# Decoder layer: GpSimd makes part of the low halves of the weights, and two more matrix products use the wide seven-product scheme

## The chip, the cores and the metric

One core of a Trainium2 chip runs the whole program. The metric is the device time of one execution, in microseconds. In the text PE is TensorE (matmul), DVE is VectorE, ACT is ScalarE, POOL is GpSimd, and SP is SyncE, which only issues transfers.

## The reference, cut to what matters

256 tokens of width 2048 go through one layer. The token mixers' part is left out here, since the change touches it in one place only.

```python
def rmsnorm(x, g):
    xf = x.astype(jnp.float32)
    y = xf * lax.rsqrt(jnp.mean(xf * xf, axis=-1, keepdims=True) + EPS)
    return (y * g.astype(jnp.float32)).astype(x.dtype)
...
h = rmsnorm(x, attn_norm[l])
proj = h @ w_in[l]
...
y_gla = (o_gla * jax.nn.silu(gr)) @ w_br_gla[l]
y_sb = stick_breaking_mixer(...) @ w_br_sb[l]
y_mem = memory_mixer(q_m, m_k, m_v) @ w_br_mem[l]
g = jax.nn.sigmoid(gates.reshape(B, T, N_BRANCH, D))
merged = g[:, :, 0] * y_gla + g[:, :, 1] * y_sb + g[:, :, 2] * y_mem
x = x + merged @ w_o[l]
h2 = rmsnorm(x, ffn_norm[l])
gate, up = jnp.split(h2 @ w_gate_up[l], 2, axis=-1)
x = x + (jax.nn.silu(gate) * up) @ w_down[l]
```

The feed-forward width is 5632. All inputs are float32, and so are the results.

## The kernel before

**High and low parts.** A matmul of float32 takes its operands rounded to fp32r. To keep the precision, every operand is split into a high part and a low part (`split`, L148): ACT casts `hi` (L151), and DVE subtracts it from the source to give `lo` (L152). A product is then three matmuls, high by high, high by low and low by high (`mm`, L268, L270, L271 in `sgemm`; L224 to L226 in `gemm`). The weights arrive as raw tiles of four chunks (a chunk is 128 of the inner dimension; the tile is 128x2048, 1024 KB). They are split two chunks at a time, 128x1024, into a pair of tiles `wh` and `wl`. From the output projection on there are six such pairs, handed out in turn (`parts`), and a pair comes free when PE has used it.

**The wide product.** `sgemm` (L233) computes two blocks of 512 columns for both halves of the tokens. The first two raw tiles of each block, 8 chunks of inner dimension, go through a scheme of seven products instead of eight (a form of Strassen's): sums of token operands are made ahead (`make_forms`, the "forms" `sh`/`sl` or `sd`), and sums of weight tiles on the way. `p` says how many chunks of a tile take part: with `p` of 4 all of them, with 2 half, and the other half goes through plain `rest` steps (the lists `l21`, `l11`, `l22`, `l12`). A unit of a product is two chunks: one split, and 2 x 3 matmuls. A `rest` step is also one split of two chunks, and 2 x 2 x 3 matmuls, for both token halves. So for each chunk in the scheme seven products of three matmuls stand where eight would.

The seven products are named by one letter in the table `seq`, which sets the order of work: `a` (p1, tile 21), `b` (p2, tile 11), `e` (p3, tile 12), `f` (q4, tile 11 after tile 21 was added to it), `g` (p5, tile 21 minus or plus 22), `h` (p6, plus 12), `i` (p7, tile 22 after 12 was added to it). `r0` and `r1` are the `rest` steps of the two blocks. The sums that change the tile in place for a product are DVE's (L283); those for `f` and `i` are transfers that accumulate, issued on POOL's queue (L331, L351), if `moved` is set and the product is not `late`. `late` is for a product whose token operand has just been made: the forms are waited for at `(made,)`, behind some of the rests, and `f`'s sum is DVE's.

**What sets the order elsewhere.** Small tasks (transposes of new operands, making of forms) are generators in a list `background`; `step` advances the first of them once behind each unit. The framework then orders each engine's queue; each engine runs its queue in order and waits on the others by semaphores.

**The places that matter.** The memory branch's result comes back from DRAM through `fetch_out` (L668), beside the small matmuls for `gaT` (L990, L994). The output projection `w_o` is two `sgemm` calls (L1110); it makes `x2` (L1116), which is transposed (L457) and split into `hh` and `hl` (L154, L155), and the forms of these are made (L420, L152). Eleven gate-and-up groups (L1142) and six calls for the down projection (L1169) follow, in three parts: groups 0 to 3, 4 to 7, 8 to 10, each part with two down calls. The first gate group has `p` of 2 and is `late`; the last down call (`end`) has `p` of 2. The down forms `sd` are made beside the third group of a part. Results of down calls but the last two are added to `x2d` in DRAM by POOL's accumulating transfers (L1177); the last two add to `x2s` in SBUF and go out (L1183, L1185).

Of the kernel before, what the change touches and what calls it, by code (L numbers as in the profile page):

```python
# [77 lines left out]
def trunk(ctx: ExitStack, tc: tile.TileContext, a, out):  # L78
# [68 lines left out]

    def split(hi, lo, src, scale=None):  # L148

        if scale is None:  # L150
            act.copy(hi, src)  # L151
            dve.tensor_tensor(lo, src, hi.bitcast(F32), op=ALU.subtract)  # L152
        else:
            act.activation(hi, src, AF.Copy, scale=scale)  # L154
            dve.scalar_tensor_tensor(lo, src, scale, hi.bitcast(F32), op0=ALU.mult, op1=ALU.subtract)  # L155
# [76 lines left out]

    def sgemm(xs, forms, w, blks, p, row0=0, late=False, moved=True, base=None, end=False):  # L233

# [37 lines left out]

        def half(raw, g):
            wh, wl = (x[:].rearrange("p (k n) -> p k n", k=2) for x in parts())
            split(wh, wl, raw[:, g : g + 2])
            return wh, wl

        def prod(dst, left, b, last, *sums):

            for g in range(0, p, 2):  # L280
                for to, of in sums:
                    x, y = (q[i][0][:, g : g + 2] for i in (to, of))
                    dve.tensor_tensor(x, x, y, op=ALU.add)  # L283
                wh, wl = half(q[b][0], g)
                for i in range(2):
                    mm(dst, left[g + i], wh[:, i], wl[:, i], last and g + i == p - 1)
                step()
# [72 lines left out]
        def rest(j, k, last):  # L360
# [4 lines left out]
            raw, g, done = loaded[j, k]  # L365
            wh, wl = half(raw, g)
            if done:
# [13 lines left out]
        if late == "forms":  # L381
            seq = [a, *l21, *r1[:1], b, *l11, *r0, *r1[1:2], (made,), g, *l22, h, e, *l12, *r1[2:3], i, f, *r1[3:]]
        elif late:
            seq = [a, *l21, b, *l11, *r0, *r1[:1], (made,), g, *l22, *r1[1:2], h, e, *l12, *r1[2:3], i, f, *r1[3:]]
        elif end:
            seq = [a, *l21, *r0, g, h, *l22, b, *l11, e, *l12, i, f, *r1]
        else:
            seq = [a, *l21, *r0[:2], g, *r0[2:], h, *l22, b, *l11, e, *l12, *r1[:2], i, *r1[2:3], f, *r1[3:]]
# [282 lines left out]
    def fetch_out(o, place):  # L671
        high, low = place

        def work():
# [3 lines left out]
            yield  # L678
            for c in range(0, 8, 4):
                split(high[:, c : c + 4], low[:, c : c + 4], v[:, c : c + 4])  # L680
                if c == 4:
                    done()
                yield
# [304 lines left out]
    for k, x in enumerate(xs):  # L988
        for i in range(2):
            pe.matmul(p[: 2 * GR, :T], w_ga[:, k], x[i], start=k + i == 0, stop=(k, i) == (KD - 1, 1))  # L990
        if k % 8 == 7:
            step()
    gaT = gl.tile([2 * GR, T], F32, name="gaT", bufs=1)
    dve.tensor_copy(gaT[:], p[: 2 * GR, :T])  # L994
    flush()
    background.append(steps)
# [108 lines left out]
    for n0 in range(0, D, 2 * NB):  # L1105
        xr = []
        for n in (n0, n0 + NB):
            xr.append(gog.tile([P, 2, NB], F32, name="xr", tag="g_og"))
            nc.sync.dma_start(xr[-1][:], a["x"][:, n : n + NB].rearrange("(t p) n -> p t n", p=P))
        for j, result in sgemm(ms, sm_, a["w_o"], (n0 // NB, n0 // NB + 1), SP, late=n0 == 0):  # L1110
            if x2 is None:
# [27 lines left out]
    for part in (range(0, 4), range(4, 8), range(8, NF)):  # L1139
        fs, tiles = [], []  # L1140
        for i in part:
            for j, result in sgemm(hs, sf, a["w_gate_up"], (i, NF + i), 4 if i else 2, late=i == 0):  # L1142
                if j == 0:
# [21 lines left out]
        for n0 in range(0, D, 2 * NB):  # L1165
            blks = (n0 // NB, n0 // NB + 1)
            end = final and n0 + 2 * NB == D
            base = (lambda j: x2s[1][:, n0 + j * NB : n0 + (j + 1) * NB]) if final else None
            for j, result in sgemm(  # L1169
                fs, sd, a["w_down"], blks, 2 if end else SP, row0=4 * part[0], moved=end, base=base, end=end  # L1170
            ):
                n = n0 + j * NB
# [63 lines left out]
```

## Time and profile before

| | us |
|---|---|
| median of 3 runs | 1610.74 (1610.11 to 1611.36) |
| the profiled execution | 1611.44 |
| its span, first to last instruction | 1609.7 |
| PE busy | 1600.1 |
| DVE busy | 1363.9 |
| ACT busy | 1046.8 |
| POOL busy | 73.9 |

The profile is of one execution, and the granted TensorE clock was 1.0 throughout. A row of a group gives the line, engine, operation, output and inputs with shapes and the count, then the busy time, the mean of one in ns, and the engine's idle time before them with what ended it. A row of waits gives who waited for whom: us in total, times, the longest. A row of the timeline gives start, length, engine, line, operation, operands and, in brackets, the idle time before it and what ended it. A matmul's length there is that of its way through a pipeline; the next one starts well before it ends.

### The profile page before, as it was taken

Reading aid. Unit: us, or ns where it says so; the run is one execution under the profiler, and the core shown is the slowest. Engines: PE = TensorE matmul, PEld = TensorE weight load, DVE = VectorE, ACT = ScalarE, POOL = GpSimd, SP = SyncE. Lnnn points to the kernel's source line nnn. Section 1 sums busy time; section 2 is a strip of 40 time slices with the busy share of each in tenths; the row PEclk is TensorE's granted clock in tenths of the full one; section 3 lists DMA queues with packets and bytes.
Section 4 is the critical chain, followed back from the end, with each engine's and each line's share of the span. In section 5 each row is a group of like instructions: output and inputs, shape, how many; then the busy total and the mean of one; then the engine's idle time right before and its main releaser. Section 6 shows DMA issues by size and latency. Waiting matters only on the chain.

```text
span 1609.7 us, 19426 instructions
## 1 busy us (share of the span) xinstructions
PE 1600.1 (99%) x7198; PEld 1313.7 (82%) x7198; DVE 1363.9 (85%) x1555; ACT 1046.8 (65%) x1279; POOL 73.9 (5%) x96
## 2 busy tenths in 40 slices
PE   9999999999999999999999999999999999999998
PEld 6888888888788888888888888888888888888887
DVE  6788788887676788987799998988878988888997
ACT  7666677776665666665656766666666666666663
POOL 0000000000000000000000000000000000110000
PEclk9999999999999999999999999999999999999999
DMA  9766768767555887887757768787898786897684
GB/s 382 286 233 212 239 216 261 208 186 256 196 176 187 290 262 248 279 281 288 241 183 259 272 231 253 259 249 235 257 280 261 227 272 232 253 277 248 190 315 130
DMA packets 66527, 394.71 MB, mean 245 GB/s; under 512 B 7360, under 2 KB 14144, under 8 KB 21632
## 3 DMA queue, kind: packets, MB, share of 16 engines
q1 hardware_dynamic: 50928, 322.92, 52.4%
q0 software_dynamic: 11936, 67.11, 21.7%
q10 hardware_dynamic: 3568, 3.44, 0.7%
q8 instruction: 56, 0.92, 0.2%
q14 instruction: 39, 0.32, 0.1%
HBM read 324.24 MB, written 12.58 MB: 209 GB/s over the span
## 4 chain that ended last, share of the span: by engine, by line
PE 95%; DMA 2%; DVE 1%; ACT 1%; issue 0%; ACTq 0%; DVEq 0%; POOLq 0%
PE acc L268 19%; PE acc L271 19%; PE acc L270 19%; PE tmp L271 7%; PE tmp L270 7%; PE tmp L268 7%; PE acc L225 4%; PE acc L226 4%; PE acc L224 4%; PE tmp L457 2%; DMA raw<-in_w_down 1%; DMA raw<-raw 1%; DMA raw<-in_w_br_mem 0%; DVE wl L152 0%; PE tmp L697 0%; PE tmp L725 0%
## 5 line engine op out<-in xcount | busy, mean ns | idle before, releaser
L152 DVE TENSOR_TENSOR wl<-raw,wh 128x1024 fp32r<-128x1024 f32 (+1 forms) x768 | 923.6, 1221 | 199.5 <-ACT wh L151 185.5
L151 ACT CAST wh<-raw 128x1024 fp32r<-128x1024 f32 (+1 forms) x769 | 799.9, 1051 | 443.8 <-PE acc L271 239.3
L268 PE MATMUL acc<-wh,xTh 128*128 128x512 f32 x532 | 210.9, 397 | 0.2 <-ACT acc L314 0.2
L271 PE MATMUL acc<-wh,xTl 128*128 128x512 f32 x532 | 207.6, 391 | 0.0
L270 PE MATMUL acc<-wl,xTh 128*128 128x512 f32 x532 | 207.5, 390 | 0.0
L268 PE MATMUL acc<-wh,hh 128*128 128x512 f32 x452 | 178.9, 396 | 0.0
L270 PE MATMUL acc<-wl,hh 128*128 128x512 f32 x452 | 176.1, 390 | 0.0
L271 PE MATMUL acc<-wh,hl 128*128 128x512 f32 x452 | 175.2, 390 | 0.0
L283 DVE TENSOR_TENSOR raw<-raw 128x1024 f32<-128x1024 f32 x136 | 164.7, 1221 | 1.6 <-DMA raw<-in_w_down 0.9
L224 PE MATMUL acc<-wh,oh 128*128 128x512 f32 x320 | 126.2, 396 | 1.5 <-ACT wh L151 1.5
L225 PE MATMUL acc<-wl,oh 128*128 128x512 f32 x320 | 125.2, 391 | 0.8 <-DVE wl L152 0.8
L226 PE MATMUL acc<-wh,ol 128*128 128x512 f32 x320 | 125.3, 391 | 0.2 <-DVE ol L152 0.2
L268 PEld LDWEIGHTS acc<-wh,xTh 128*128 128x128 f32 x532 | 100.0, 188 | 23.0 <-ACT acc L314 3.2
L268 PE MATMUL tmp<-wh,sh 128*128 128x512 f32 x300 | 118.1, 394 | 0.0
L271 PE MATMUL tmp<-wh,sl 128*128 128x512 f32 x300 | 117.2, 391 | 0.0
L271 PEld LDWEIGHTS acc<-wh,xTl 128*128 128x128 f32 x532 | 99.9, 188 | 21.0
L270 PE MATMUL tmp<-wl,sh 128*128 128x512 f32 x300 | 117.0, 390 | 0.0
L270 PEld LDWEIGHTS acc<-wl,xTh 128*128 128x128 f32 x532 | 100.0, 188 | 19.8
L268 PEld LDWEIGHTS acc<-wh,hh 128*128 128x128 f32 x452 | 84.9, 188 | 18.6 <-ACT acc L314 1.0
L271 PEld LDWEIGHTS acc<-wh,hl 128*128 128x128 f32 x452 | 84.9, 188 | 17.9
L270 PEld LDWEIGHTS acc<-wl,hh 128*128 128x128 f32 x452 | 85.0, 188 | 16.7
L268 PE MATMUL acc<-wh,fh 128*128 128x512 f32 x220 | 86.8, 394 | 0.4 <-ACT acc L314 0.4
(305 smaller groups left out, 2228.6 us busy)
## 6 DMA issues: line engine op xcount, KB each, us to landing
raw<-in_w_gate_up SPq DMA_DIRECT2D x88, 1024.0 KB, 6.8
raw<-in_w_in SPq DMA_DIRECT2D x56, 1024.0 KB, 6.1
raw<-raw POOLq DMA_DIRECT2D x52, 1024.0 KB, 8.0
raw<-in_w_gate SPq DMA_DIRECT2D x48, 1024.0 KB, 7.3
raw<-in_w_down SPq DMA_DIRECT2D x44, 1024.0 KB, 6.9
raw<-in_w_o SPq DMA_DIRECT2D x16, 1024.0 KB, 5.4
raw<-in_w_mem_kv SPq DMA_DIRECT2D x14, 1024.0 KB, 9.9
raw<-in_w_br_mem SPq DMA_DIRECT2D x8, 1024.0 KB, 5.4
```

Source lines behind the costliest of these rows:

```text
L151: act.copy(hi, src)
L152: dve.tensor_tensor(lo, src, hi.bitcast(F32), op=ALU.subtract)
L224: pe.matmul(o[t][:], xh[:, s], wh[:, j], start=k == 0, stop=False)
L225: pe.matmul(o[t][:], xh[:, s], wl[:, j], start=False, stop=False)
L226: pe.matmul(o[t][:], xl[:, s], wh[:, j], start=False, stop=k == nk - 1)
L268: pe.matmul(dst[:], xh, wh, start=id(dst) not in begun, stop=False, skip_group_check=True)
L270: pe.matmul(dst[:], xh, wl, start=False, stop=False, skip_group_check=True)
L271: pe.matmul(dst[:], xl, wh, start=False, stop=last, skip_group_check=True)
L283: dve.tensor_tensor(x, x, y, op=ALU.add)
L457: pe.transpose(dst, src, ident)
```

## The change

Six edits:

1. `split` can have the low part made by another engine, and POOL makes it in two cases. With `third` set (the `w_o` calls, all gate groups, all down calls), it makes the first of the two low parts of each plain rest tile. With `third="more"` (the last down call) it also makes the second low part of `b`, `e` and `f`.
2. The first gate group and the last down call have `p` of 4 instead of 2. Their lists `l21` to `l12` are then empty.
3. In the first gate group (`late="later"`) two rests of the second block stand ahead of `(made,)`, where one stood.
4. The first of the last two down calls (12 chunks) gets an order of its own: `g` before the rests `r0`, and one rest between `i` and `f`. Also, its sum for `f` is now POOL's transfer (`moved=final`).
5. `fetch_out` splits in three pieces of 2, 2 and 4 columns of 256 instead of two of 4.
6. The loop for `gaT` steps the background behind every fourth `k` instead of every eighth, and does not empty it behind.

```diff
-    def split(hi, lo, src, scale=None):
+    def split(hi, lo, src, scale=None, by=dve):
         if scale is None:
             act.copy(hi, src)
-            dve.tensor_tensor(lo, src, hi.bitcast(F32), op=ALU.subtract)
+            by.tensor_tensor(lo, src, hi.bitcast(F32), op=ALU.subtract)
...
         def prod(dst, left, b, last, *sums):
-                wh, wl = half(q[b][0], g)
+                wh, wl = half(q[b][0], g, nc.gpsimd if third == "more" and g and b in (11, 12) else dve)
...
         def rest(j, k, last):
-            wh, wl = half(raw, g)
+            wh, wl = half(raw, g, nc.gpsimd if third and g == 0 else dve)
...
         elif late:
-            seq = [a, *l21, b, *l11, *r0, *r1[:1], (made,), g, *l22, *r1[1:2], h, e, *l12, *r1[2:3], i, f, *r1[3:]]
+            m = 2 if late == "later" else 1
+            seq = [a, *l21, b, *l11, *r0, *r1[:m], (made,), g, *l22, *r1[m:2], h, e, *l12, *r1[2:3], i, f, *r1[3:]]
         elif end:
             seq = [a, *l21, *r0, g, h, *l22, b, *l11, e, *l12, i, f, *r1]
+        elif nk < 4 * SP:
+            seq = [a, *l21, g, *r0, h, *l22, b, *l11, e, *l12, *r1[:1], i, *r1[1:], f]
         else:
             seq = [a, *l21, *r0[:2], g, *r0[2:], h, *l22, b, *l11, e, *l12, *r1[:2], i, *r1[2:3], f, *r1[3:]]
...
-            for c in range(0, 8, 4):
-                split(high[:, c : c + 4], low[:, c : c + 4], v[:, c : c + 4])
-                if c == 4:
+            for c, e in ((0, 2), (2, 4), (4, 8)):
+                split(high[:, c:e], low[:, c:e], v[:, c:e])
+                if e == 8:
...
-        if k % 8 == 7:
+        if k % 4 == 3:
             step()
...
-    flush()
     background.append(steps)
...
-        for j, result in sgemm(ms, sm_, a["w_o"], (n0 // NB, n0 // NB + 1), SP, late=n0 == 0):
+        for j, result in sgemm(ms, sm_, a["w_o"], (n0 // NB, n0 // NB + 1), SP, late=n0 == 0, third=True):
...
-            for j, result in sgemm(hs, sf, a["w_gate_up"], (i, NF + i), 4 if i else 2, late=i == 0):
+            for j, result in sgemm(hs, sf, a["w_gate_up"], (i, NF + i), SP, late="" if i else "later", third=True):
...
-                fs, sd, a["w_down"], blks, 2 if end else SP, row0=4 * part[0], moved=end, base=base, end=end
+            how = dict(moved=final, base=base, end=end, third="more" if end else True)
+            for j, result in sgemm(fs, sd, a["w_down"], blks, SP, row0=4 * part[0], **how):
```

The line numbers of the changed kernel are a few higher: the low part stays L152, and L268, L270, L271, L283, L331, L351, L420, L457, L1116, L1150 become L272, L274, L275, L287, L335, L355, L427, L464, L1123, L1157. The built programs hold 6660 matmuls with 512 columns before and 6648 now. DVE's low parts of 128x1024 go from 766 to 697, and POOL has 75; DVE's sums go from 136 to 139. On PE the order between the first gate group and the last down calls is unchanged.

DVE's queue in the first gate group, before, from the reduction over x2's squares on. `wl` are low parts of the gate's weights (7835 of a rest, 7763 of the plain half of tile 11), `hl` those of the new operand, `rs` the steps of its norm, `cv` a form being made:

```order
L1125 TENSOR_REDUCE s2_7655<-x2_ss_6934 128x2
L152 TENSOR_TENSOR wl_7835<-raw_7832,wh_7834 128x1024
L160 TENSOR_SCALAR rs_m_7658<-s2_7655 128x2
L155 SCALAR_TENSOR_TENSOR hl_6932<-tmp_7714,vecs_85,hh_6931 128x256
L162 TENSOR_SCALAR rs_h_7660<-rs_m_7658 128x2
L152 TENSOR_TENSOR wl_7763<-raw_7750,wh_7762 128x1024
L164 TENSOR_SCALAR rs_i_7662<-rs_h_7660 128x2
L155 SCALAR_TENSOR_TENSOR hl_6932<-tmp_7714,vecs_85,hh_6931 128x256
```

The same place now, where the low parts of a rest (7807) and of `b`'s first half (7751), with a result of `w_o` between and one behind them, have just gone by:

```order
L155 SCALAR_TENSOR_TENSOR hl_6936<-tmp_7718,vecs_85,hh_6935 128x256
L287 TENSOR_TENSOR raw_7706<-raw_7706,raw_7910 128x1024
L1132 TENSOR_REDUCE s2_7659<-x2_ss_6938 128x2
L155 SCALAR_TENSOR_TENSOR hl_6936<-tmp_7718,vecs_85,hh_6935 128x256
L160 TENSOR_SCALAR rs_m_7662<-s2_7659 128x2
L155 SCALAR_TENSOR_TENSOR hl_6936<-tmp_7737,vecs_85,hh_6935 128x256
L162 TENSOR_SCALAR rs_h_7664<-rs_m_7662 128x2
L427 TENSOR_TENSOR cv_7822<-hh_6935,hl_6936 128x512
L164 TENSOR_SCALAR rs_i_7666<-rs_h_7664 128x2
L155 SCALAR_TENSOR_TENSOR hl_6936<-tmp_7737,vecs_85,hh_6935 128x256
L168 SCALAR_TENSOR_TENSOR rs_t_7668<-rs_i_7666 128x2
L152 TENSOR_TENSOR wl_7761<-raw_7748,wh_7760 128x1024
```

`b`'s second low part, 7761, now stands behind a sum for `g` and four `hl`; before, the part at its place, 7763, stood behind one.

DVE's queue where the last gate group ends and the first of the last two down calls begins, before. L406 and L1150 make the group's `up` result, which PE transposes next:

```order
L316 TENSOR_TENSOR cv_12635<-cv_12460,tmp_12357 128x512
L152 TENSOR_TENSOR wl_12726<-raw_12713,wh_12725 128x1024
L152 TENSOR_TENSOR wl_12746<-raw_12743,wh_12745 128x1024
L283 TENSOR_TENSOR raw_12713<-raw_12713,raw_12784 128x1024
L406 TENSOR_TENSOR cv_12633<-acc_12355,cv_12633 128x512
L152 TENSOR_TENSOR wl_12769<-raw_12743,wh_12768 128x1024
L1150 SCALAR_TENSOR_TENSOR cv_12696<-acc_12354,r2_7657,cv_12675 128x512
L406 TENSOR_TENSOR cv_12635<-acc_12356,cv_12635 128x512
L152 TENSOR_TENSOR wl_12788<-raw_12713,wh_12787 128x1024
L1150 SCALAR_TENSOR_TENSOR cv_12697<-cv_12635,r2_7657,cv_12676 128x512
```

And now:

```order
L320 TENSOR_TENSOR cv_12648<-cv_12473,tmp_12370 128x512
L287 TENSOR_TENSOR raw_12726<-raw_12726,raw_12756 128x1024
L152 TENSOR_TENSOR wl_12739<-raw_12726,wh_12738 128x1024
L152 TENSOR_TENSOR wl_12760<-raw_12726,wh_12759 128x1024
L287 TENSOR_TENSOR raw_12726<-raw_12726,raw_12756 128x1024
L413 TENSOR_TENSOR cv_12646<-acc_12368,cv_12646 128x512
L287 TENSOR_TENSOR raw_12726<-raw_12726,raw_12823 128x1024
L1157 SCALAR_TENSOR_TENSOR cv_12709<-acc_12367,r2_7661,cv_12688 128x512
L413 TENSOR_TENSOR cv_12648<-acc_12369,cv_12648 128x512
L152 TENSOR_TENSOR wl_12778<-raw_12726,wh_12777 128x1024
L1157 SCALAR_TENSOR_TENSOR cv_12710<-cv_12648,r2_7661,cv_12689 128x512
```

Three low parts and three sums stand between the first and the last of these rows, where four low parts and one sum stood. The tile in the first sum (12784, now 12756) was the fourth of the call's loads in SP's queue and is now the second.

POOL's queue at the end, before, from the fetch of `x2s` on (the transfer rows L351 and L331 are the accumulations for `i` and `f`):

```order
L1163 DMA x2s_12703<-x2d_6933 128x2048
L1163 DMA x2s_12704<-x2d_6933 128x2048
L351 DMA raw_12784<-raw_12810 128x2048
L351 DMA raw_13034<-raw_13049 128x1024
L331 DMA raw_13080<-raw_12971 128x1024
```

And now, from the second row of these on. 12792 and 12895, 13009 and 13185 are of rests, 13105 of `b`, 13126 of `e`, 13169 of `f`:

```order
L355 DMA raw_12756<-raw_12823 128x2048
L152 TENSOR_TENSOR wl_12792<-raw_12789,wh_12791 128x1024
L335 DMA raw_12849<-raw_12726 128x2048
L152 TENSOR_TENSOR wl_12895<-raw_12892,wh_12894 128x1024
L152 TENSOR_TENSOR wl_13009<-raw_13006,wh_13008 128x1024
L355 DMA raw_13040<-raw_13066 128x2048
L152 TENSOR_TENSOR wl_13105<-raw_13092,wh_13104 128x1024
L335 DMA raw_13092<-raw_12983 128x2048
L152 TENSOR_TENSOR wl_13126<-raw_13066,wh_13125 128x1024
L152 TENSOR_TENSOR wl_13169<-raw_13092,wh_13168 128x1024
L152 TENSOR_TENSOR wl_13185<-raw_13182,wh_13184 128x1024
```

The accumulation for `f` in the last call (now 13092) waits for POOL's own low part 13105, moves all four chunks instead of two, and is waited for by POOL's 13169, with 13185 queued behind that.

More of the change, by code (lines that the diff above doesn't have):

```diff
@@ L231, in gemm, with sgemm @@
         return o
-    def sgemm(xs, forms, w, blks, p, row0=0, late=False, moved=True, base=None, end=False):
+    def sgemm(xs, forms, w, blks, p, row0=0, late=False, moved=True, base=None, end=False, third=False):
         nk = len(xs)
@@ L271, in mm, with half @@
             pe.matmul(dst[:], xl, wh, start=False, stop=last, skip_group_check=True)
-        def half(raw, g):
+        def half(raw, g, by=dve):
             wh, wl = (x[:].rearrange("p (k n) -> p k n", k=2) for x in parts())
-            split(wh, wl, raw[:, g : g + 2])
+            split(wh, wl, raw[:, g : g + 2], by=by)
             return wh, wl
@@ L1168, in trunk @@
             base = (lambda j: x2s[1][:, n0 + j * NB : n0 + (j + 1) * NB]) if final else None
-            for j, result in sgemm(
-                fs, sd, a["w_down"], blks, 2 if end else SP, row0=4 * part[0], moved=end, base=base, end=end
-            ):
+            how = dict(moved=final, base=base, end=end, third="more" if end else True)
+            for j, result in sgemm(fs, sd, a["w_down"], blks, SP, row0=4 * part[0], **how):
                 n = n0 + j * NB
```

## The prediction

> **What bounds the kernel now.** I read the page first: busy times and the chain that ended last.
>
> ```profile
> PE 1600.1 (99%) x7198; PEld 1313.7 (82%) x7198; DVE 1363.9 (85%) x1555; ACT 1046.8 (65%) x1279; POOL 73.9 (5%) x96
> ...
> PE 95%; DMA 2%; DVE 1%; ACT 1%; issue 0%; ACTq 0%; DVEq 0%; POOLq 0%
> ```
>
> TensorE (PE) is busy 99% and makes 95% of the chain, so only two things shorten the program: fewer matmuls, or fewer waits of PE. A matmul's mean of about 0.39 us is its length in the pipeline, not its price; that comes from the windows (busy us and count of PE, PEld, DVE, ACT, POOL; then clock, DMA share, GB/s):
>
> ```profile
> 600.00:650.00 50.00, 50.00 (x222) 41.24 (x221) 41.71 (x40) 31.75 (x35) 1.73 (x2) 1.00 0.83 269
> 826.00:1605.00 779.00, 777.83 (x3484) 640.82 (x3483) 693.04 (x716) 500.48 (x569) 46.56 (x57) 1.00 0.77 246
> 914.00:937.00 23.00, 23.00 (x111) 19.01 (x110) 22.96 (x50) 15.88 (x27) 2.54 (x4) 1.00 0.43 150
> 1004.00:1046.00 42.00, 42.00 (x191) 34.73 (x190) 40.88 (x45) 27.63 (x33) 0.86 (x1) 1.00 0.75 254
> 1571.00:1604.00 33.00, 32.56 (x144) 26.28 (x143) 25.60 (x27) 12.85 (x14) 1.73 (x2) 1.00 0.43 124
> ```
>
> In the first, a stretch without a wait, 222 matmuls take 50.00 us: 0.225 us each at full clock. The others are the stage from the output projection on (DVE 693 of 779 us), the first gate group's turn from x2 to the forms (DVE full), a gate group beside which the down forms are made, and the last down block.
>
> Then the waits, PE's and ACT's:
>
> ```profile
> PE tmp L457 <- DVE cv L1150: 0.7, 1, 0.7
> PE acc L268 <- ACT acc L314: 0.6, 2, 0.4
> PE tmp L856 <- DVE gaT L994: 0.3, 1, 0.3
> PE acc L226 <- DVE ol L152: 0.2, 1, 0.2
> ...
> ACT wh L151 <- PE acc L271: 239.3, 279, 3.7
> ...
> ACT wh L151 <- DMA raw<-raw: 8.3, 4, 3.3
> ```
>
> Behind the program's start, PE waits for other engines under 2 us in all. ACT waits 239 us for PE to free buffers: high and low parts are made as far ahead as there are buffers. So work taken off DVE earns nothing in general; it counts at the few places where PE waits.
>
> **The change part by part.** The prices first: DVE's low part and its sum, the only row in which GpSimd (POOL) writes a tile, the accumulating transfers by size, and the landing of the last of them, issued at 1584.0.
>
> ```profile
> L152 DVE TENSOR_TENSOR wl<-raw,wh 128x1024 fp32r<-128x1024 f32 x402 | 482.9, 1223 | 76.9 <-ACT wh L151 70.0
> L283 DVE TENSOR_TENSOR raw<-raw 128x1024 f32<-128x1024 f32 x84 | 101.8, 1221 | 1.4 <-DMA raw<-in_w_down 0.9 <-DMA raw<-in_w_gate_up 0.2
> L922 POOL MEMSET ra<- 128x512 f32 x2 | 1.1, 526 | 92.5 <-PE tmp L457 51.0 <-DVE gr L782 41.6
> raw<-raw POOLq DMA_DIRECT2D x52, 1024.0 KB, 8.0
> raw<-raw POOLq DMA_DIRECT2D x4, 512.0 KB, 5.2
> DMA to landing us min/median/max: 4.5/4.5/4.5
> ```
>
> *Matmuls.* In two products the unit goes from two chunks by seven to four by seven. Two chunks more save one product of three matmuls each: 6 per call, 12 in all. 12 x 0.225 = **-2.7**. This term has one answer, and no wait lies between it and the end.
>
> *Low parts on GpSimd.* The order shows 75 on POOL and 697 of 128x1024 on DVE, where 766 stood; 6 of these 772 and 3 of DVE's sums are new. No row shows POOL doing a subtraction. Its memset writes 512 in 0.526 us, so 1024 in 1.05; if two inputs and the output each cost that, 3.2. I take 2.1, the middle, since the memset is a third of the work at best. Most are of plain rests: 12 matmuls, 2.7 us of PE, each. There are six pairs of high and low buffers, so a part may be started five parts ahead, 6.8 us if all are of products (1.35 us each) and more with rests; cast 1.05 and low part 2.1 fit. Price in the rests **0** (if that cover were gone, 2.1 - 1.2 = 0.9 each). DVE is relieved of 66 operations; by ACT's row that is free time and not a gain. While a part waits for its cast on POOL, the transfers queued behind it wait: the accumulations, for which ACT's next casts wait (8.3 us in four of 56 so far, never PE), and `x2d`, which nothing needs before the last part.
>
> [...]
>
> *Smaller chunks when the memory branch comes back.*
>
> ```profile
> 428.25 2.59 DVE L152 TENSOR_TENSOR ol<-raw,oh 128x1024 fp32r<-128x1024 f32 x2
> ...
> 428.89 0.40 PE L225 MATMUL acc<-wl,oh 128*128 128x512 f32 x1
> 429.52 0.50 PE L226 MATMUL acc<-wh,ol 128*128 128x512 f32 x1 [0.23 <-DVE ol L152]
> ...
> 430.56 0.40 PE L224 MATMUL acc<-wh,oh 128*128 128x512 f32 x1
> ...
> 431.22 1.12 PE L856 MATMUL tmp<-rb,gaT 32*128 32x512 f32 x2 [0.26 <-DVE gaT L994]
> ```
>
> L226 starts 0.63 after L225 (0.40 lost), L856 0.66 after L224 (0.43 lost). The fetch is now issued at the first of four steps and not of two, 8 matmuls of 0.11 earlier (0.9 us), and the first low part is half as wide. Both gaps close: **-0.8** (0 if the transfer, or ACT's casts, come last).
>
> *Start of the last down blocks.*
>
> ```profile
> 1534.20 0.69 DVE L316 TENSOR_TENSOR cv<-cv,tmp 128x512 f32<-128x512 f32 x1
> ...
> 1539.15 1.23 DVE L283 TENSOR_TENSOR raw<-raw 128x1024 f32<-128x1024 f32 x1 [0.94 <-DMA raw<-in_w_down]
> ...
> 1544.00 0.48 PE L268 MATMUL tmp<-wh,sd 128*128 128x512 f32 x1
> 1544.41 0.74 DVE L1150 SCALAR_TENSOR_TENSOR cv<-cv,r 128x512 f32<-128x512 f32 x1
> 1545.21 0.87 PE L457 MATMUL tmp<-cst,cv 128*128 128x128 f32 x6 [0.74 <-DVE cv L1150]
> ```
>
> PE loses 1.21 - 0.225 = 0.99 us here, waiting for the last `u`. Between L316 and this L1150 DVE did four low parts and one sum; the new order has three and three, one more (1.13 from start to start), but the tile that the sum waited 0.94 for is now second in the load queue instead of fourth, and the 0.96 that DVE waited for a cast there is filled. `u` comes some 0.4 earlier and PE asks one matmul (0.2) later: **-0.6** (0 to -1.0). In the same call `f`'s sum becomes a transfer of 8.0; `e`, two rests and `i` (2.7 each, 10.8) stand between `b` and `f`, so **0**, and 1 to 2 if it landed last.
>
> *First gate group.* Sums double (late, so all on DVE), in DVE's full stretch:
>
> ```profile
> 914.37 0.39 PE L268 MATMUL tmp<-wh,hh 128*128 128x512 f32 x1
> 914.57 0.69 DVE L406 TENSOR_TENSOR cv<-acc,cv 128x512 f32<-128x512 f32 x1
> ...
> 919.25 0.16 DVE L160 TENSOR_SCALAR rs_m<-s 128x2 f32<-128x2 f32 x1
> 919.33 0.47 DVE L155 SCALAR_TENSOR_TENSOR hl<-tmp,vecs,hh 128x256 fp32r<-128x256 f32 x1
> ```
>
> By the new order the second low part of `b` stands behind two low parts and a sum (1.13 each), three operations of 0.6, four `hl` (0.4) and five tiny ones (0.07): 7.1 us after 914.5, done at 922.9. PE asks for it after 28 matmuls (6.3) and 16 transposes (1.6) from 914.37: 922.3. A new wait of **+0.6** (0 to +3). The forms are asked for after the same 96 matmuls as before, since one more rest stands ahead of them.
>
> *End block.* The accumulation that `f` needs is 1024 KB instead of 512, and its last reader is a POOL low part. From the end of the rest that frees the buffer to `f`'s second half, PE has 66 matmuls, 14.9 us. The chain: cast 1.05, POOL 2.1, issue to landing, two casts 2.1, POOL 2.1. With 6.5 for the landing (between 4.5, the half-size one here at 1584, and the 8.0 median) 13.9; the rest's part next on POOL makes 16.0 against 16.2. With 8.0, 1.3 late; with POOL at 3.2 too, 4.5 late. I take **+0.7** (0 to +4.5).
>
> Sum: -2.7 - 0.8 - 0.6 + 0.6 + 0.7 = -2.8 on the profiled execution's 1611.44 (span 1609.7 and 1.7 around it), that is 1608.6. The median of the runs is 0.7 below that execution: **1607.9**.
>
> **The rivals.** The bound for "no change" is 0.2%, 3.2 us, about what a measurement of this kernel can tell.
>
> *No new waits.* Both positive terms are bounded by 0, since POOL took three DVE parts ahead of the full stretch and may take under 2.1 us. All gaps close: -2.7 - 0.8 - 1.0 = -4.5, and 1611.44 - 4.5 - 0.7 = **1606.2**. For: PE's waits are so short now. Against: DVE's 22.96 of 23.00.
>
> *DVE and POOL shut each other out.* If an operation with two SBUF inputs on one holds up those on the other, each moved part takes 2.1 from DVE and gives back 1.13. In all, 75 x 2.1 - 66 x 1.13 = 83 us of the 86 that DVE has free. Place: where DVE has no slack. First gate group, three parts, +3 instead of +0.6; end block, five parts in 33 us with 25.6 busy, +2.5; second w_o block +1; three groups with down forms (40.88 of 42) +0.5 each: 8.0 - 4.1 = +3.9, **1614.6**. It decides for slower once POOL's part holds DVE over about 2 us. For: nothing in this trace, POOL never computes there beside a full DVE. Against: in most groups the parts are far ahead.
>
> [...]
>
> *A low part stuck in POOL's queue* behind transfers that wait for a result (x2d in the down blocks): the third rest's part is asked for 10 us into a block, the transfers before it issue within 4, so mostly covered; 0.5 in each of four blocks gives 1609.9.
>
> **How the numbers follow.** Forecast 0.44, no new waits 0.30, shut out 0.18, queue 0.08. Faster by over 0.2% (below 1607.5): 0.28 of the second and 0.10 of the first, 0.38. Slower (above 1614.0): 0.12 of the third and 0.02 of the first, whose unknown terms can reach +7.5 together, 0.14. The same: 0.32 of the first, 0.08 of the queue, 0.06 of the third and 0.02 of the second, 0.48. The forecast's own range is 1606.5 to 1611.5. Low end: the second case without the 0.6 that PE loses for ACT's copy, 1605.6; high end 1614.0, which leaves out the upper part of the third case and little else.
>
> **What would show it.** Right: 6648 instead of 6660 matmuls of 512; no PE wait on gaT or ol; under 0.5 on L1157's `u`; new waits of PE on DVE's or POOL's `wl` about 918 to 923 and in the last 15 us; POOL's parts near 2.1 us. Wrong: DVE's two-input operations longer than 1.22 beside POOL (the lock), or PE waits in the plain gate groups (cover gone), or no new wait at all.

## The result, and the profile after

The changed kernel takes 1689.31 us (median of 5 runs, 1684.74 to 1689.65) against 1610.74: ratio 1.0481, 95% interval 1.0470 to 1.0493. The prediction was 1607.9, with a range up to 1614.0. So the change makes the kernel 78.6 us slower where a gain of 2.8 was forecast. The profiled execution took 1689.31, its span is 1687.5.

The page of the changed kernel first: busy times, then the low parts of DVE and of POOL (count, busy us, mean ns, idle before them). The last row is DVE's low part on the page of the kernel before.

```profile
PE 1626.4 (96%) x7186; PEld 1325.2 (79%) x7186; DVE 1410.8 (84%) x1491; ACT 1053.6 (62%) x1287; POOL 282.6 (17%) x172
...
L152 DVE TENSOR_TENSOR wl<-raw,wh 128x1024 fp32r<-128x1024 f32 (+1 forms) x699 | 912.0, 1321 | 225.7 <-ACT wh L151 214.6
...
L152 POOL TENSOR_TENSOR wl<-raw,wh 128x1024 fp32r<-128x1024 f32 x75 | 209.4, 2792 | 388.7 <-ACT wh L151 294.4
```

```profile
L152 DVE TENSOR_TENSOR wl<-raw,wh 128x1024 fp32r<-128x1024 f32 (+1 forms) x768 | 923.6, 1221 | 199.5 <-ACT wh L151 185.5
```

Two things are to be seen. PE has the 12 matmuls less (7186 for 7198), yet 26 us more of busy time, so its matmuls got longer. And DVE did 64 operations less but was busy 47 us longer: its low part went from 1221 ns to 1321 on the mean. POOL's takes 2.79 us on the mean, not the 2.1 assumed.

The three largest of PE's waits behind it (us in total, times, the longest):

```profile
PE tmp L464 <- DVE cv L1157: 36.4, 11, 3.7
PE acc L272 <- ACT acc L318: 5.7, 5, 1.4
PE acc L274 <- POOL wl L152: 2.4, 2, 1.7
```

Only 2.4 us are spent waiting for a part that POOL made. The 36.4 are the transposes of the gate groups' `u`, the result of a group that PE transposes next; DVE makes it in two operations, one for each half of the tokens. There are eleven waits, one at the end of each group, nine of them alike. One of the nine, first in DVE's queue:

```profile
1012.92 1.22 DVE L287 TENSOR_TENSOR raw<-raw 128x1024 f32<-128x1024 f32 x1
1014.23 3.27 DVE L152 TENSOR_TENSOR wl<-raw,wh 128x1024 fp32r<-128x1024 f32 x1
1017.42 0.68 DVE L413 TENSOR_TENSOR cv<-acc,cv 128x512 f32<-128x512 f32 x1
1018.02 1.21 DVE L152 TENSOR_TENSOR wl<-raw,wh 128x1024 fp32r<-128x1024 f32 x1
1019.16 0.74 DVE L1157 SCALAR_TENSOR_TENSOR cv<-acc,r,cv 128x512 f32<-128x512 f32 x1
1019.82 0.68 DVE L413 TENSOR_TENSOR cv<-acc,cv 128x512 f32<-128x512 f32 x1
1020.41 1.21 DVE L152 TENSOR_TENSOR wl<-raw,wh 128x1024 fp32r<-128x1024 f32 x1
1021.55 2.83 DVE L1157 SCALAR_TENSOR_TENSOR cv<-cv,r 128x512 f32<-128x512 f32 x1
```

The same stretch in POOL's queue, and then in PE's:

```profile
1012.96 3.46 POOL L152 TENSOR_TENSOR wl<-raw,wh 128x1024 fp32r<-128x1024 f32 x1 [9.64 <-ACT wh L151]
1016.35 0.87 POOL L355 DMA_DIRECT2D raw<-raw  x1
1020.85 2.98 POOL L152 TENSOR_TENSOR wl<-raw,wh 128x1024 fp32r<-128x1024 f32 x1 [3.63 <-ACT wh L151]
```

```profile
1020.35 0.40 PE L274 MATMUL acc<-wl,hh 128*128 128x512 f32 x1
1024.43 0.44 PE L464 MATMUL tmp<-cst,cv 128*128 128x128 f32 x2 [3.68 <-DVE cv L1157]
```

DVE's low part at 1014.23 ends at 1017.50, 1.08 behind the end of POOL's part at 1016.42. The second `u`, begun at 1021.55, ends at 1024.38, 0.55 behind the end of POOL's at 1023.83. Both were held until POOL was done, and from there took 1.08 and 0.55, somewhat less than they take alone (1.22 and 0.74). So 3.27 - 1.22 = 2.05 and 2.83 - 0.74 = 2.09 were lost, 4.14 in all. POOL seems to be held likewise: its part at 1020.85 began beside DVE's low part and ended 2.21 behind the end of that one at 1021.62. No part of POOL's runs beside the first `u`, which has one input in PSUM (`acc`) and takes 0.74; the one such `u` that has a part beside it, in the last group, takes 0.75.

How much of that DVE could afford is in the trace of before, at the same place, in DVE's queue and PE's:

```profile
1002.64 0.75 DVE L1150 SCALAR_TENSOR_TENSOR cv<-cv,r 128x512 f32<-128x512 f32 x1
```

```profile
1003.69 0.49 PE L457 MATMUL tmp<-cst,cv 128*128 128x128 f32 x3
```

The second `u` ended at 1003.39 and was asked for at 1003.69. The lead was 0.30 us, there and in the other eight of the nine groups; 4.14 - 0.30 = 3.84, and PE lost 3.85 (from 1020.35 + 0.225 to 1024.43).

Behind the wait comes a second loss. Windows of the changed kernel, on four stretches of 3.41 us: PE's busy time and count, granted clock, DMA share, GB/s.

```profile
1018.68:1022.09 3.41, 2.02 (x9) 1.00 1.15 192
1022.09:1025.50 3.41, 1.07 (x6) 1.00 0.80 250
1025.50:1028.92 3.42, 3.42 (x11) 0.50 0.59 163
1028.92:1032.33 3.41, 3.41 (x18) 1.00 0.58 245
```

About 1.1 us after PE had its input, its clock was halved for 3.42 us. The trace holds twelve such stretches in its body, seven of 3.41 us and five of 6.83, 58 us in all, so up to 29 us of full-speed work were lost. Before, there was none.

### The profile page after: what moved, and what is told of

The parts are those of the page before. It is cut to its first block, busy times and chain, and to the rows that moved or that the text cites. A ratio compares the mean times of both kernels' runs of the same rounds, so it can differ in the third digit from the quotient of the medians.

```text
span 1687.5 us, 19503 instructions
## 1 busy us (share of the span) xinstructions
PE 1626.4 (96%) x7186; PEld 1325.2 (79%) x7186; DVE 1410.8 (84%) x1491; ACT 1053.6 (62%) x1287; POOL 282.6 (17%) x172
## 3 DMA queue, kind: packets, MB, share of 16 engines
q10 hardware_dynamic: 3568, 3.44, 0.6%
## 5 line engine op out<-in xcount | busy, mean ns | idle before, releaser
L152 DVE TENSOR_TENSOR wl<-raw,wh 128x1024 fp32r<-128x1024 f32 (+1 forms) x699 | 912.0, 1321 | 225.7 <-ACT wh L151 214.6
L152 POOL TENSOR_TENSOR wl<-raw,wh 128x1024 fp32r<-128x1024 f32 x75 | 209.4, 2792 | 388.7 <-ACT wh L151 294.4
L272 PE MATMUL acc<-wh,xTh 128*128 128x512 f32 x532 | 210.6, 396 | 0.2 <-ACT acc L318 0.2
L274 PE MATMUL acc<-wl,xTh 128*128 128x512 f32 x532 | 207.5, 390 | 0.0
L275 PE MATMUL acc<-wh,xTl 128*128 128x512 f32 x532 | 207.4, 390 | 0.0
L287 DVE TENSOR_TENSOR raw<-raw 128x1024 f32<-128x1024 f32 x139 | 181.0, 1310 | 2.8 <-DMA raw<-in_w_gate 1.5
L272 PE MATMUL acc<-wh,hh 128*128 128x512 f32 x440 | 178.8, 407 | 4.6 <-ACT acc L318 2.8
L274 PE MATMUL acc<-wl,hh 128*128 128x512 f32 x440 | 177.0, 402 | 0.8 <-POOL wl L152 0.8
L275 PE MATMUL acc<-wh,hl 128*128 128x512 f32 x440 | 176.8, 405 | 0.0
L272 PE MATMUL tmp<-wh,sh 128*128 128x512 f32 x306 | 120.3, 393 | 0.0
L274 PE MATMUL tmp<-wl,sh 128*128 128x512 f32 x306 | 119.6, 391 | 0.3 <-DVE wl L152 0.3
L275 PE MATMUL tmp<-wh,sl 128*128 128x512 f32 x306 | 119.5, 391 | 0.0
L272 PEld LDWEIGHTS acc<-wh,xTh 128*128 128x128 f32 x532 | 99.9, 188 | 23.1 <-ACT acc L318 3.3
L275 PEld LDWEIGHTS acc<-wh,xTl 128*128 128x128 f32 x532 | 99.9, 188 | 20.9
L274 PEld LDWEIGHTS acc<-wl,xTh 128*128 128x128 f32 x532 | 100.0, 188 | 19.9
L355 POOL DMA_DIRECT2D raw<-raw x32 | 28.2, 880 | 479.4 <-DVE raw L287 250.0
L272 PEld LDWEIGHTS acc<-wh,hh 128*128 128x128 f32 x440 | 85.5, 195 | 22.8 <-ACT acc L318 3.6
L275 PEld LDWEIGHTS acc<-wh,hl 128*128 128x128 f32 x440 | 86.8, 197 | 18.8
```

The lines of the kernel that those rows point to most:

```text
L152: by.tensor_tensor(lo, src, hi.bitcast(F32), op=ALU.subtract)
L272: pe.matmul(dst[:], xh, wh, start=id(dst) not in begun, stop=False, skip_group_check=True)
L274: pe.matmul(dst[:], xh, wl, start=False, stop=False, skip_group_check=True)
L275: pe.matmul(dst[:], xl, wh, start=False, stop=last, skip_group_check=True)
L355: nc.gpsimd.dma_start(q[22][0][:, :p], q[12][0][:, :p], accum_op=ALU.add)
```

## The experiments

Unless a sentence says otherwise, each is the changed kernel with one edit. Ratios are to the kernel before on the same chip.

**All low parts on DVE.**

```diff
-            wh, wl = half(raw, g, nc.gpsimd if third and g == 0 else dve)
+            wh, wl = half(raw, g, dve)
```

(and the same in `prod`).

> The changed kernel with all 75 low parts of GpSimd made by VectorE again; four chunks by seven, the new order and the smaller fetch chunks stay. If GpSimd's subtractions are the cause (by shutting VectorE out, or by being late), the 3.85 us waits of TensorE at the gate groups' ends and the half-clock stretches go, and what is left is the rest of the change, predicted at -2.7 - 0.8 - 0.6 + 0.6: 1605 to 1612 us. If the new order and the larger products are the cause, VectorE has 75 operations of 1.22 more to do at the same places, the waits stay and it takes 1680 us or more.

Measured: 1615.36 us (1613.66 to 1617.48), ratio 1.0028 (1.0018 to 1.0039). So POOL's parts cost 1689.3 - 1615.4 = 73.9 of the 78.6. The stage from the output projection on, in one window of this run (us of PE, PEld, DVE, ACT, POOL, then clock, DMA share, GB/s), and in one of the changed kernel:

```profile
826.00:1612.00 786.00, 777.78 (x3476) 638.79 (x3474) 703.03 (x728) 505.67 (x575) 47.37 (x58) 1.00 0.78 248
```

```profile
825.00:1687.00 862.00, 805.38 (x3474) 653.01 (x3472) 740.52 (x652) 506.43 (x575) 255.15 (x133) 0.97 0.73 226
```

PE's idle time is 56.6 with POOL's parts and 8.2 without: 48.4 of waits. Its busy time differs by 27.6, the half clock. Together they are the 76.0 by which the windows differ in length; the spans differ by 74.5, so the windows' ends don't match by 1.5. The clock of 1.00 in the first row also says that without POOL's parts there is no half clock. What is left above the expected 1605 to 1612 lies in other edits (below).

**POOL's rests alone, in the kernel before.**

```diff
-            wh, wl = half(raw, g)
+            wh, wl = half(raw, g, nc.gpsimd if third and g == 0 else dve)
```

(and `third` as in the changed kernel.)

> The kernel before with nothing but the rests' first low part of a pair moved to GpSimd (72 of them from the output projection on; products stay two by seven where they were, order and fetch as before). If GpSimd's subtractions are the cause, at least nine tenths of the 78 us appear here too: 1675 to 1695 us. If the order and larger products are the cause, or needed for it, 1609 to 1620 us.

Measured: 1679.53 us (1678.51 to 1682.08), ratio 1.0427 (1.0413 to 1.0442): 68.6 more than before, with no other edit. That is within the range expected, though a little under nine tenths of the 78. The waits for `u` are there too:

```profile
PE tmp L457 <- DVE cv L1150: 34.7, 11, 3.7
```

**POOL subtracts, and nobody reads it.** `w_o` keeps its parts on DVE here.

```diff
-            split(wh, wl, raw[:, g : g + 2], by=by)
+            split(wh, wl, raw[:, g : g + 2])
+            if by is nc.gpsimd:
+                spare(wh, raw[:, g : g + 2])
...
+    def spare(wh, src):
+        v = scr[:].rearrange("p (k n) -> p k n", k=2)
+        nc.gpsimd.tensor_tensor(v, src, wh.bitcast(F32), op=ALU.subtract)
```

> From the gate groups on VectorE makes every low part, and GpSimd subtracts the same two inputs at the same 67 places into a spare tile that nothing reads. Lock theory: GpSimd's operation shuts VectorE's two-input operations out for its length no matter who uses the result, and VectorE is not relieved either, so the waits at the gate groups' ends are 3.8 us or longer and the time is 1685 us or more (up to 1740). Late-parts theory (TensorE waits because a part comes 2.8 us after its cast instead of 1.3): nothing waits for the spare tile, 1605 to 1615 us.

Measured: 1702.81 us (1697.85 to 1705.52), ratio 1.0560 (1.0541 to 1.0579). The theory that the parts come late falls: PE waits for none of these, and the time is 87 above the run without them. The second `u` (group rows: busy us, mean ns) here and, in the second fence, with all parts on DVE:

```profile
L1164 DVE SCALAR_TENSOR_TENSOR cv<-cv,r 128x512 f32<-128x512 f32 x12 | 26.6, 2225 | 0.0
L1164 DVE SCALAR_TENSOR_TENSOR cv<-acc,r,cv 128x512 f32<-128x512 f32 x10 | 7.4, 740 | 0.0
```

```profile
L1157 DVE SCALAR_TENSOR_TENSOR cv<-cv,r 128x512 f32<-128x512 f32 x12 | 8.9, 745 | 0.0
```

The second `u`, with two inputs in SBUF, takes 2225 ns on the mean; nine of the twelve stand beside a subtraction. The form with one input in PSUM takes 740, but only one of the ten stands beside a subtraction (0.75 us), so these rows don't compare the two forms; the run with the sum in PSUM does.

**POOL only writes.** As the run before, with a copy of one element per partition and two memsets in place of the subtraction.

```diff
+    def spare(wh, src):
+        nc.gpsimd.tensor_copy(scr[:, :1], wh[:, 0, :1].bitcast(F32))
+        for _ in range(2):
+            nc.gpsimd.memset(scr[:], 0.0)
```

> As the run with the spare subtraction, but GpSimd, after a copy of one element per partition of the same high part, only writes the spare tile twice (two memsets of 128x1024, some 2.1 us by the memset row). Lock theory, in which it is the reading of the second input that is shared: VectorE's operations keep 1.22 us, no 3.85 us waits, within 5 us of the run without GpSimd's parts. If it is enough that GpSimd is busy or writes SBUF, VectorE's operations are stretched to 2 us or more beside it and the time is 1660 us or more.

Measured: 1615.83 us (1614.80 to 1617.12), ratio 1.0031 (1.0019 to 1.0043), 0.5 from the run without POOL's parts. Its page and DVE's groups:

```profile
L422 POOL COPY scr<-wh 128x1 f32<-128x1 f32 x67 | 119.8, 1788 | 224.2 <-ACT wh L151 223.9
...
L424 POOL MEMSET scr<- 128x1024 f32 x134 | 129.3, 965 | 7.6
```

```profile
L152 DVE TENSOR_TENSOR wl<-raw,wh 128x1024 fp32r<-128x1024 f32 (+1 forms) x774 | 929.2, 1220 | 200.4 <-ACT wh L151 186.7 <-PE tmp L471 1.9 <-issue 0.3
```

POOL is busy for 129 us of writing beside DVE, and DVE's low part keeps 1220 ns. So it isn't POOL's writing, or its being busy, that shuts DVE out; what the subtraction has beyond these is its reading of two whole tiles. The copy shows the other direction: one column takes 0.2 us at best and 1.79 on the mean, which fits that it waits for DVE.

**The first rest of each call on DVE.** 56 parts stay on POOL.

```diff
-            wh, wl = half(raw, g, nc.gpsimd if third and g == 0 else dve)
+            wh, wl = half(raw, g, nc.gpsimd if third and g == 0 and (j, k) != (0, 2 * SP) else dve)
```

> The changed kernel with one GpSimd part in four given back to VectorE: the first rest of each call, whose part lies beside the last u of the call before. Lock theory with this place: in the trace the second u takes 2.83 instead of 0.74 only because that part runs, so each of ten waits shrinks from 3.85 by 2.1 to about 1.75 (the stretched low part 8 us earlier still counts) and, being short, no longer brings the half clock, which costs 25: 1635 to 1655 us. If what counts is the number of parts (19 of 75 given back), a quarter of the 74 us between this kernel and the one with all on VectorE: 1670 us.

Measured: 1634.83 us (1633.65 to 1635.66), ratio 1.0147 (1.0132 to 1.0163), just under the range expected. A quarter of the parts, 19 of 75, made three quarters of the loss: 54.5 of 73.9. (There are nine waits of 3.85, not ten as written there.) Two of the old waits, 3.1 us each, stayed: in those groups another part slid beside the `u`.

```profile
PE tmp L464 <- DVE cv L1157: 8.4, 4, 2.9
```

**The last sum in PSUM.** All 75 parts stay on POOL.

```diff
+                        if (t, j) in c and bank:
+                            dve.tensor_tensor(o[t, j][:], o[t, j][:], c[t, j][:], op=ALU.add)
...
-dve.scalar_tensor_tensor(u[t], result(t), r2
+dve.scalar_tensor_tensor(u[t], result(t, bank=True), r2
```

> The changed kernel with all 75 parts on GpSimd, but the sum ahead of the second u is written back to PSUM instead of SBUF, so that this u reads one input from SBUF and not two. Lock theory (two SBUF inputs on VectorE against a reader on GpSimd): the second u takes 0.75 beside GpSimd's part, the waits at the gate groups' ends shrink by 2.1 to about 1.75 and the half clock there goes: 1635 to 1655 us. If VectorE is shut out whatever its inputs are, or the part is merely late, the u still takes 2.8 and the time stays at 1680 us or more.

Measured: 1650.14 us (1648.81 to 1651.69), ratio 1.0241 (1.0227 to 1.0255): 39.2 less than the changed kernel, with not one part moved. DVE's queue at the same boundary, with POOL's part running from 1016.00 to 1019.03:

```profile
1015.58 1.21 DVE L152 TENSOR_TENSOR wl<-raw,wh 128x1024 fp32r<-128x1024 f32 x1
1016.71 0.73 DVE L1159 SCALAR_TENSOR_TENSOR cv<-acc,r,cv 128x512 f32<-128x512 f32 x1
1017.37 2.80 DVE L429 TENSOR_TENSOR cv<-fh,fl 128x512 f32<-128x512 f32 x2
```

The `u` now passes beside POOL's part in 0.73, and the hold falls on the next operation with two SBUF inputs, for which PE does not wait then. The waits at the group ends went to about 1.5 in most groups, from the low part or the sum that is held earlier (here a sum, 3.32 us from 1008.21), and all but one of the half-clock stretches in the body went with them. DVE lost about as much in all as before (113 us above the lengths that its operations have alone, against 119), so what these 39.2 us hang on is the place of the hold and not its amount.

**Matmuls in the wait.** 15 matmuls whose result is overwritten, ahead of the transposes of each `u`.

```diff
+            for _ in range(0 if c else fill):
+                pe.matmul(p[:], hh[:, 0, :P], hh[:, 0:2].rearrange("p k t -> p (k t)"), start=True, stop=True)
```

> The changed kernel with 15 more matmuls of 512 (3.4 us), whose result is overwritten, ahead of the transposes of each u: TensorE works through most of the 3.85 us in which it otherwise waits. If the half clock follows from TensorE's idle time, the stretches of 3.4 and 6.8 us at half clock behind ten of these waits go, which gives back 25, and the two groups without a long wait cost up to 3.4 each: 1662 to 1672 us. If the half clock has another cause (the other engines' work, or a limit that more matmuls only make worse), the time stays at 1687 us or rises to 1700.

Measured: 1676.18 us (1675.92 to 1676.54), ratio 1.0403 (1.0388 to 1.0417): 165 matmuls more and 13.1 us less. It came out above the 1672 expected because the waits that the 37 us of matmuls fill shrank by about 2.65 of 3.4 each (to 1.2). The second `u` is still held, but the clock stays (columns as above):

```profile
1019.00:1025.00 6.00, 4.95 (x27) 3.88 (x25) 6.00 (x6) 0.80 (x3) 1.86 (x1) 1.00 0.71 218
1025.00:1060.00 35.00, 35.00 (x157) 28.95 (x155) 34.38 (x32) 24.05 (x27) 10.54 (x4) 1.00 0.69 236
```

One stretch of half clock is left in the body, at 926.7, ahead of the first gate group's end. So the half clock follows from PE's idle time.

**Each part as two halves.** Two operations of 128x512.

```diff
-            by.tensor_tensor(lo, src, hi.bitcast(F32), op=ALU.subtract)
+            for x in range(2) if by is nc.gpsimd else ():
+                by.tensor_tensor(lo[:, x], src[:, x], hi[:, x].bitcast(F32), op=ALU.subtract)
+            if by is dve:
+                by.tensor_tensor(lo, src, hi.bitcast(F32), op=ALU.subtract)
```

> The changed kernel with each GpSimd part done as two operations of 128x512 instead of one of 128x1024. If the lock is held for one instruction and given to the one that waits, a VectorE operation waits for half a part at most: the second u ends 1.1 earlier, the low part 8 us ahead of it is stretched by 1.0 less, and ten waits of 3.85 shrink to between 1.7 and 2.8; the half clock goes with them in part or whole: 1640 to 1668 us. If GpSimd keeps VectorE out across both halves, the time stays at 1685 us or more.

Measured: 1665.44 us (1659.80 to 1671.63), ratio 1.0339 (1.0312 to 1.0366). The time is within what was expected, the waits are not: eight of them still take about 3.5 us. DVE's queue at a boundary:

```profile
1002.02 2.24 DVE L155 TENSOR_TENSOR wl<-raw,wh 128x1024 fp32r<-128x1024 f32 x1
1004.18 0.68 DVE L416 TENSOR_TENSOR cv<-acc,cv 128x512 f32<-128x512 f32 x1
1004.78 1.72 DVE L155 TENSOR_TENSOR wl<-raw,wh 128x1024 fp32r<-128x1024 f32 x1
1006.42 0.74 DVE L1160 SCALAR_TENSOR_TENSOR cv<-acc,r,cv 128x512 f32<-128x512 f32 x1
1007.08 0.68 DVE L416 TENSOR_TENSOR cv<-acc,cv 128x512 f32<-128x512 f32 x1
1007.68 2.28 DVE L155 TENSOR_TENSOR wl<-raw,wh 128x1024 fp32r<-128x1024 f32 x1
1009.88 1.75 DVE L1160 SCALAR_TENSOR_TENSOR cv<-cv,r 128x512 f32<-128x512 f32 x1
```

The hold does end with each instruction (the low part at 1002.02 ended at 1004.26, while POOL's second half ran from 1003.14 to 1005.42), but where two parts held two operations, by 2.05 and 2.09, their four halves now hold four, by 1.02, 0.50, 1.06 and 1.01. In a queue without slack that is nearly the same. What is gained lies elsewhere: PE's waits for ACT's copy went from 5.7 us to 2.4 in all, and the half-clock stretches from 58 us to 34.

**One part per call.** Only the low part of the third rest of the first half stays on POOL, 17 parts; `prod` has all of its low parts on DVE.

```diff
-            wh, wl = half(raw, g, nc.gpsimd if third and g == 0 else dve)
+            wh, wl = half(raw, g, nc.gpsimd if third and (j, k) == (0, 3 * SP) else dve)
```

> The changed kernel with one part per call left on GpSimd (the third rest of the first half, 17 parts), the others on VectorE. If place decides, a part in the middle of a call, where VectorE is 11 to 15% free over a group, costs nothing: 1614 to 1617 us, as with none; up to 1622 if it slides next to the last u in two groups, as in the run with the first rest given back. If every part costs what it takes from VectorE (2.26 held, 1.22 given back), 17 x 1.04 = 17.7 more than with none: 1633 us.

Measured: 1621.84 us (1619.89 to 1623.61), ratio 1.0074 (1.0057 to 1.0091): 6.5 above none, 0.38 a part instead of 1.04. The longest wait for `u` that is left in its trace is 0.22, but the 1614 to 1617 expected of a place that costs nothing was missed. The two largest of its waits are in the stretch around the first gate group (1.36 and 1.83 at 920.8 and 967.7, with one half-clock stretch); from 937 to 970 DVE is busy 32.97 of 33.00. So place decides nearly all, but not one of the tried places of POOL's parts earned anything.

**The last down blocks' edits alone**, in the kernel before, all parts on DVE.

```diff
-                fs, sd, a["w_down"], blks, 2 if end else SP, row0=4 * part[0], moved=end, base=base, end=end
+                fs, sd, a["w_down"], blks, SP, row0=4 * part[0], moved=final, base=base, end=end
```

(and the branch for `nk < 4 * SP`).

> The kernel before with the last down blocks' edits alone: four chunks by seven in the last block, the transfers instead of the sums in the last part's calls, the new order of its pieces, and every low part on VectorE. By the offsets of TensorE between the run with all parts on VectorE and the kernel before (4.72 us behind ahead of these blocks, 3.32 at the end) these edits are worth -1.4: 1609 to 1610 us, ratio 0.9985 to 0.9997. If they are worth what was predicted without GpSimd in the end block (-1.35 of matmuls, -0.6, up to -0.6), 1608.5; if they cost, 1611 us or more.

Measured: 1611.92 us (1610.85 to 1613.28), ratio 1.0006 (0.9997 to 1.0015), a miss. TensorE is 0.27 ahead of the kernel before when these blocks begin and 1.10 behind at the end: +1.4, where the same edits made -1.4 in the run with all parts on DVE. What has grown is a wait of PE's for ACT, from 0.43 us to 2.37. ACT's queue:

```profile
1569.20 1.05 ACT L151 CAST wh<-raw 128x1024 fp32r<-128x1024 f32 x1 [1.10 <-PE acc L271]
1576.07 1.04 ACT L151 CAST wh<-raw 128x1024 fp32r<-128x1024 f32 x1 [5.82 <-DVE raw L283]
1577.03 0.58 ACT L314 COPY acc<-tmp 128x512 f32<-128x512 f32 x1
```

The copy that PE needs stands behind a cast that waits for one of DVE's sums. From the same code, the framework put DVE's operations in another order in these two kernels (there one of the sums stands ahead of the block's results, here all stand behind them), so the gain of this edit hangs on an order that it doesn't set. Why the order differs was not tried.

**All on DVE, and the first gate group as before.**

```diff
-            for j, result in sgemm(hs, sf, a["w_gate_up"], (i, NF + i), SP, late="" if i else "later", third=True):
+            for j, result in sgemm(hs, sf, a["w_gate_up"], (i, NF + i), SP if i else 2, late=i == 0, third=True):
```

> The run with all low parts on VectorE, with the first gate group put back too (two chunks by seven there, and one rest of the second half ahead of the forms). TensorE's offset against the kernel before grows from 0.70 to 4.72 in that group and the next group's start. If those edits are the cause (three more sums and three more low parts, 7.3 us, in a stretch in which VectorE has no free time), the 4.0 go and 1611 to 1612 us are left, no slower than the kernel before by more than 0.1%. If the loss lies elsewhere, 1614 us or more.

Measured: 1612.73 us (1611.33 to 1613.73), ratio 1.0010 (1.0001 to 1.0019), 0.7 above the range expected. TensorE's offset ahead of the last blocks is 0.47 instead of 4.72, so the 4.0 did lie in the first gate group. The other 1.1 above the kernel before arise in the last blocks, where the wait of the run above is there again (2.1 us).

**The memory branch's edit alone**, in the kernel before.

```diff
-            for c in range(0, 8, 4):
+            for c, e in ((0, 2), (2, 4), (4, 8)):
...
-        if k % 8 == 7:
+        if k % 4 == 3:
...
-    flush()
```

> The kernel before with the memory branch's edit alone (first two low parts half as wide, a step every four chunks, no flush ahead of the gates' copy). Forecast: both gaps close, -0.8, 1610.4 us. By the trace of the run with all parts on VectorE: the gap on ol closes (-0.40), the one on gaT grows from 0.43 to 1.07, so +0.2, 1611.5 us. Either is within 0.1% of the kernel before, so the trace's gaps decide: no gap at the first gates' matmul, or one of about 1.07.

Measured: 1611.12 us (1610.33 to 1612.33), ratio 1.0001 (0.9992 to 1.0009). In its trace the gap on `ol` is gone and the one on `gaT` is 1.08:

```profile
PE tmp L856 <- DVE gaT L994: 0.9, 1, 0.9
```

No kernel tried here is faster than the one before.

## Why the prediction was wrong

*What bounds the kernel.* Right: PE, busy 99%, with waits of under 2 us behind the start. That is also why what delays DVE at a place without slack was paid in full: at a group's end 4.14 less the lead of 0.30, and PE lost 3.85.

*Matmuls, -2.7.* The count was right (7186 for 7198). In the times the gain can't be seen, since waits of a few us stand against it in every run that has it.

*Low parts on GpSimd, 0.* This is the step that failed. It said: "Price in the rests **0**", because a part that POOL makes in 2.1 us is made early enough for PE, and "DVE is relieved of 66 operations; by ACT's row that is free time and not a gain". The first half held: PE waited 2.4 us in all for POOL's parts. But the price of an operation on another engine was taken to be its own delay, and not what it does to the engines beside it. In the runs DVE's operations with two SBUF inputs were held while POOL subtracted (a low part took 3.27 us instead of 1.22, a second `u` 2.83 instead of 0.74). By the trace, 73 of POOL's 75 parts hold one up, which adds 119 us to the lengths of DVE's operations, where the 75 that went took 75 x 1.22 = 92 with them. The spare subtraction, the writes, and the sum in PSUM show this from three sides.

*The rival of the lock, +3.9.* The mechanism was right and its size was not. It took 2.1 per part, which is near (a `u` held in full lost 2.09), and reckoned that all this would leave DVE 83 us busier; its busy time in the stage rose by 37.5 (703.03 to 740.52). So the hold itself was not priced too low. But the rival looked for stretches in which DVE has no free time over tens of us, of which there are few. What counts is the lead of each single result that PE asks for. At the end of each gate group the last `u` had 0.30 us, and the profile of before had it in view: the prediction quoted one of these transposes waiting for `u` at 1545.21 and treated it as one place. It is eleven places, nine of them with two held operations each: 9 x 3.85 = 34.7, and 48.4 of new waits in all, where the rival had 8.0.

*The half clock.* The prediction had no term for it. 27.6 us, over a third of the loss, come behind the waits and not in them.

*Smaller chunks in the memory branch, -0.8.* Wrong, 0: the gap on `ol` closed (-0.4), but the one on `gaT` grew from 0.43 to 1.08. One wait went and the next in the same chain got longer.

*First gate group, +0.6 (0 to +3).* Too small: 4.0 in TensorE's offset. The step timed `b`'s second low part, at which there was almost no wait. But three sums and three low parts more, 6 x 1.22 = 7.3 us, went into a stretch where DVE was busy 22.96 of 23.00; they come out as waits further on (941.9 to 944, 962 to 967 and at 1007 in the run with all parts on DVE), less the 1.35 of six matmuls.

*Last down blocks, -0.6 and +0.7.* With the parts on DVE, -1.4 in one order of its queue and +1.4 in another, the matmuls counted in. The wait for `u` did go in both. The size was within the bounds that were given, but its sign is not set by the edit.

*End block, +0.7 (0 to +4.5), and the rival of the part stuck in POOL's queue.* In the down blocks of the changed kernel PE waits for one part of POOL's only, a rest's in the end block: 1.66 us, up to 1677.88. That is within the bounds, and it speaks against the rival; but no run moves the end block's parts alone, so what they cost there is not known.

## What to carry to other kernels

Work taken from VectorE to GpSimd was not work taken off VectorE here: an operation of VectorE's with two SBUF inputs was held to the end of GpSimd's subtraction (a low part took 3.27 us instead of 1.22), and GpSimd took 2.79 us on the mean for a part that takes VectorE 1.22. So first ask which VectorE operations stand beside it and what lead their results have over TensorE. A queue's free time over a stretch says nothing on that; look up the lead of each result that the bounding engine asks for, above all those that come round once in every block. And price a long wait of TensorE with what follows it: in the changed kernel the clock was at half for 3.41 or 6.83 us in twelve places, each time behind 3.41 us of which TensorE was idle for 2 us or more.

## What the runs showed of the hardware

*Who is held, and by what.* Beside POOL's subtraction DVE's operations with two SBUF inputs were held to its end (low part 1.22 to at most 3.44 us, sum 1.22 to 3.48, second `u` 0.74 to 2.83, even a step on 128x2 elements 0.16 to 2.35), and those with an input in PSUM were not (0.68 to 0.75). Beside POOL's memsets low parts and sums kept their 1.22. POOL seems to have waited for more than one instruction at times. Its longest part (5.58 us at 952.27) stood beside three of DVE's low parts in a row, and in the run where it only writes three copies of one column took 9.1 us, each beside eight low parts in a row. What lets POOL in between two of DVE's operations, as at 1021.62, no run shows. The shortest of the 75 parts took 2.35, and the one at 1020.85 ended 2.21 behind the end of DVE's low part.

*When the clock halves.* In the trace of the changed kernel all half-clock stretches begin on one grid of 3.413 us: their starts lie 27, 13, 15, 14, 13, 39, 15, 14, 13, 39 and 15 steps apart. Five traces (the changed kernel, POOL alone, the spare subtraction, the halves, the first rest) hold 1169 whole steps at full clock from 825 us on. Each matmul is counted here as busy for 0.225 us from its start, or up to the next start; the rest of a step is idle. Where PE was idle for 2.2 us or more of a step, the next was at half clock in 40 cases of 40; with 2.05 to 2.2 in 6 of 11; with less in none of 1118. So two waits of the same 3.5 us can cost differently, by where the grid cuts them: in the run with halves those at 1054.9 and 1372.1 brought none.
